# Attention opening: the keys' sine products are kept in the unused half of the rotated queries' buffer

## The chip, the cores and the metric

The kernel runs on one core of one Trainium2 chip. The metric is the device time of one execution in microseconds (us); lower is better.

## The reference

A network of two layers is computed for 256 tokens of width 1024, in fp32. The first layer mixes with a gated linear recurrence (HGRN2), the second with sparse attention (NSA); each is followed by a SwiGLU feed-forward stage, and every stage's input is modulated by the condition vector `c`. What matters here is the opening of the attention: shared keys and values are projected from one modulated input, queries from another; the selected and the window keys and all queries are normalized per head and rotated by position.

```python
def apply_rope(x, cos, sin):
    x1, x2 = jnp.split(x, 2, axis=-1)
    return jnp.concatenate([x1 * cs - x2 * sn, x2 * cs + x1 * sn], axis=-1)
...
ks = apply_rope(rms_norm(k_sel, k_norm[1]), cos, sin)
kw = apply_rope(rms_norm(k_win, k_norm[2]), cos, sin)
q = rms_norm(proj[..., :NSA_Q_WIDTH].reshape(B, S, NSA_HEADS, NSA_HEAD_DIM), q_norm)
q_rope = apply_rope(q, cos, sin)
```

## The kernel before, in words

Activations lie with features on the 128 partitions and the 256 tokens along the free axis. All weights are streamed from HBM in pieces of 1 MB: SyncE issues a load into one of four `raw` buffers (`issue`, L308) whenever one comes free. Each piece is split into two fp32r parts in `process`: ScalarE (ACT) casts the high part `wh` (L337), VectorE (DVE) subtracts to get the low part `wl` (L341); TensorE (PE) multiplies both (`mm3`, L551 to L553; `tok_steps`, L993 to L995). Activations are split in the same way into `h` high (ACT, L546) and `h` low (DVE, L547).

A rotation (`rotate`, L1260) needs x1 and x2 swapped between partitions. DVE computes a sine product into a tile `us` (L1265) and a cosine product straight into the target (L1266); four DMAs issued by GpSimd (POOL, L1269) then move `us` by 32 partitions and add it into the target. The target is `KR` for the two keys (branches 0 and 1) and `QR` for the four pairs of query projections 0 to 3, each of which fills one quarter of QR (two of its eight columns of 256 tokens). The tag `us` has two buffers; in the order of the program the users are key 0, key 1, query 0, query 1, query 2, query 3. A buffer comes free when its four DMAs are done. The names in the profile are `usk` and `usq`.

The attention stage (`nsa`, L1325) first projects the keys and values that need no later input, then builds the query input `hq` (`full_pair`, L1370), rotates the keys (L1371), and goes through the steps of `ORDER["nsa"]`: `q0` to `q3` are query projections with their rotation (`query`, L1382), `K` builds the input of the remaining values (L1408, whose `h` the values' matmuls `v` need), `c0` and `c1` the compressed blocks, `G` the gates, `R` the multiplication of KR by the keys' norms (L1323), `s0` to `s7` the scores (`attend_scores`, PE at L1584 reads QR and KR), `v0` to `v7` the products with the values, `a` parts of the modulation (`ada`, a DVE sum over a weight piece at L406).

Order of the work: the program is traced in the order above, and a planner then lays out every engine's instructions by priority and by when it reckons buffers and inputs to be free; `AHEAD` and `PRI` move steps forward or back in priority (`rot` has -75, `q0` has 80). Each engine works its list in order, so an instruction that waits holds all that stands behind it on that engine. Waits and buffer releases follow from the tiles that the instructions read and write.

Of the kernel before, what the change touches and what calls it, by code (L numbers as in the profile page):

```python
# [11 lines left out]
F32 = mybir.dt.float32  # L12
# [9 lines left out]
P = 128  # L22
S = 256
# [166 lines left out]
def first(name):  # L190

    def wrap(f):
        def g(self, *a, **k):
            n = PRI.get(name, 0)
            if not n:
                return f(self, *a, **k)
            with self.tc.high_priority(offset=n):
                return f(self, *a, **k)
        return g
    return wrap  # L200


class K:
# [1053 lines left out]
        return u, sq  # L1257

    @first("rot")
    def rotate(self, u, gain, kr, name):  # L1260

        nc = self.nc
        cs, sn = (self.c(n)[:, None, :].to_broadcast([P, 2, S]) for n in ("cos", "sin"))
        us = self.s2.tile([P, 2, S], F32, tag="us", bufs=2, name=f"us{name}")
        nc.vector.scalar_tensor_tensor(us, u, gain, sn, op0=ALU.mult, op1=ALU.mult)  # L1265
        nc.vector.scalar_tensor_tensor(kr, u, gain, cs, op0=ALU.mult, op1=ALU.mult)  # L1266
        for b in range(4):
            d, e = 32 * b, 32 * (b ^ 1)
            nc.gpsimd.dma_start(kr[d:d + 32], us[e:e + 32], accum_op=ALU.add)  # L1269
# [55 lines left out]
    def nsa(self):  # L1325
        nc = self.nc
        with self.tc.tile_pool(name="ns", bufs=1) as sp, self.tc.tile_pool(name="ns2", bufs=2) as s2, \
                ExitStack() as self.late:
            self.sp, self.s2 = sp, s2
            self.PC, self.Pt, self.RQ, self.rq = {}, {}, {}, None  # L1330
            self.rsel = sp.tile([P, 4 * P], F32R, name="rsel")
            rsel = s2.tile([P, 2, S], F32, tag="hsq", bufs=2, name="rselr").rearrange("p a b -> p (a b)")
            nc.sync.dma_start(rsel, self.a["rsel"])
            nc.scalar.copy(self.rsel, rsel)
            self.w2 = sp.tile([P, 2, 2, 64], F32, name="w2")
            nc.sync.dma_start(self.w2, self.a["w2"])

            def proj(name, i, h):
                ws = self.fetch(name, i, ahead=0)
                ps = self.acc_tile(f"{name}{i}")  # L1340
                for m in range(2):
                    self.gemm(ps[:, m], self.tiles(ws[m]), h[0], h[1])
                return ps

            KR = sp.tile([P, 2, 2, S], F32, name="KR")
            V = sp.tile([P, 2, 2, 256], F32, name="V")
            self.KR, self.V = KR, V
            Dt = [sp.tile([P, 2, 512], F32, tag=f"D{i}", name=f"D{i}") for i in range(2)]
            with ExitStack() as early:
                sk = early.enter_context(self.tc.tile_pool(name="nsk", bufs=1))  # L1350
                dk = []
                for kind in range(2):
                    dk.append(self.gemm_deferred(self.fetch("kv", kind), self.h, sk, f"kv{kind}", 3))
                kk = []
                for br in range(2):
                    sw, u = self.gemm_deferred(self.fetch("kv", 2 + 2 * br), self.h, sk, f"k{br}", 3)
                    sq = s2.tile([P, 2, S], F32, tag="hsq", bufs=2, name=f"hsqk{br}")
                    hu = s2.tile([P, 2, S], F32, tag="hu", bufs=2, name=f"huk{br}")
                    for m in range(2):
                        nc.scalar.activation(sq[:, m], u[:, m], AF.Square, bias=sw[:, m:m + 1])  # L1360
                        nc.scalar.activation(hu[:, m], u[:, m], AF.Identity, bias=sw[:, m:m + 1])
                    kk.append((hu, sq))
                self.load_late()
                while self.n_proc <= SCHED.index(("lin", "nq", 0)):
                    self.process()
                xr = sk.tile([P, KD, S], F32, name="xr")
                for m in range(0, KD, 2):
                    nc.vector.tensor_tensor(xr[:, m:m + 2], self.x[:, m:m + 2],
                                            self.rstd[:, None, :].to_broadcast([P, 2, S]), op=ALU.mult)
                hq = self.full_pair(1, 2, xr, s2, QACT)  # L1370
                for br in range(2):  # L1371
                    self.rotate(kk[br][0], self.col("k_norm", 1 + br), KR[:, :, br], f"k{br}")
                ks = [KR[:, :, br] for br in range(2)]
                rs = self.head_norm(kk)
                for kind in range(2):
                    self.cmp_blocks(*dk[kind], kind, Dt[kind], sk)
                self.QR = sp.tile([P, 8, S], F32, name="QR")

                self.QN, self.O, hk = {}, None, []
                qq, qd = {}, []  # L1380

                def query(i):  # L1382
                    if i == 2:
                        qd.append(sp.tile([P, 2, 2, S], F32, tag="D0", name="qd"))
                    qq[i] = self.raw_heads(proj("nq", i, hq), f"q{i}", qd[0][:, i % 2] if i > 1 else None)
                    self.rotate(qq[i][0], self.col("q_norm"), self.QR[:, 2 * i:2 * i + 2], f"q{i}")

                def query_norm(g):
                    pairs = [qq.pop(2 * g), qq.pop(2 * g + 1)]
                    self.QN[g] = [u for u, _ in pairs]  # L1390
                    self.row_norm(pairs, g)

                def values(br):
                    ps = self.acc_tile(f"v{br}")
                    self.gemm_tok(ps, hk[0], self.fetch("kv", 3 + 2 * br, ahead=0))
                    nc.scalar.copy(V[:, :, br], ps)

                comp = self.compress(Dt)
                for t in ORDER["nsa"]:
                    n = int(t[1:] or 0)  # L1400
                    ahead = AHEAD.get(t, 0)
                    with self.tc.high_priority(offset=ahead) if ahead else ExitStack():
                        if t[0] == "q":
                            query(n)
                        elif t[0] == "R":
                            self.head_mul(*rs, kk, ks)
                        elif t[0] == "K":
                            hk.append(self.full_pair(0, "kv", xr, s2, KACT))  # L1408
                            early.close()
                            self.s3 = self.late.enter_context(self.tc.tile_pool(name="nsp", bufs=PTS))  # L1410
                        elif t[0] == "G":
                            self.gates(hq)
                        elif t[0] == "c":
                            next(comp)
                        elif t[0] == "n":
                            query_norm(n)
                        elif t[0] == "w":
                            values(n)
                        elif t[0] == "x":
                            self.cmp_softmax(n)  # L1420
                        elif t[0] == "s":
                            self.attend_scores(n)
                        elif t[0] == "v":
                            if self.O is None:
                                self.O = self.h_tiles(0)
                            self.attend_values(n)
                        else:
                            self.adas(1)
            gate = self.need(("gate", 2))
            nxt = self.next_h(1, 3)  # L1430
            for i in range(4):
                ws = self.fetch("nsa_out", i)
                for m in range(2):
                    ps = self.acc_tile(f"nso{i}_{m}")
                    self.gemm_wide(ps, self.tiles(ws[m]), lambda k: self.h0[:, k, :, :S])
                    self.residual(ps[:, 0], 2 * i + m, gate, nxt, ps[:, 1])
            self.end_residual(nxt)
            self.h = nxt
# [331 lines left out]
```

## Time and profile before

| | us |
|---|---|
| median of 3 runs (lowest to highest) | 716.28 (715.77 to 716.33) |
| the profiled execution | 716.71 |
| its span | 714.9 |
| PE busy in the span | 696.8 |
| DVE busy in the span | 585.5 |
| ACT busy in the span | 429.6 |
| POOL busy in the span | 20.0 |

The span is the time from the first to the last recorded instruction of the profiled execution; 1.8 us of its time lie outside. PE stands for TensorE's matmuls, PEld for its weight loads, DVE for VectorE, ACT for ScalarE, POOL for GpSimd, SP for SyncE. A line is written L1265. Tiles carry the names of the program; `us` of the keys is `usk`, of the queries `usq`. The granted clock (PEclk) is the share of full speed that TensorE was given. The attention stage lies between about 357 and 500 us of the span.

### The profile page before, as it was taken

Reading aid. Unit: us, or ns where it says so; the run is one execution under the profiler, and the core shown is the slowest. Engines: PE = TensorE matmul, PEld = TensorE weight load, DVE = VectorE, ACT = ScalarE, POOL = GpSimd, SP = SyncE. Lnnn points to the kernel's source line nnn. Section 1 sums busy time; section 2 is a strip of 40 time slices with the busy share of each in tenths; the row PEclk is TensorE's granted clock in tenths of the full one; section 3 lists DMA queues with packets and bytes.
Section 4 is the critical chain, followed back from the end, with each engine's and each line's share of the span. In section 5 each row is a group of like instructions: output and inputs, shape, how many; then the busy total and the mean of one; then the engine's idle time right before and its main releaser. Section 6 shows DMA issues by size and latency. Waiting matters only on the chain.

```text
span 714.9 us, 13853 instructions
## 1 busy us (share of the span) xinstructions
PE 696.8 (97%) x5429; PEld 608.1 (85%) x5429; DVE 585.5 (82%) x1216; ACT 429.6 (60%) x855; POOL 20.0 (3%) x29
## 2 busy tenths in 40 slices
PE   7999999999999999999998599999999999999998
PEld 4998987999998888888897598555899888888887
DVE  6996986799999999999696589875899887686651
ACT  4669977667564665634375366779757665654330
POOL 0000000000000000000003130100000000000000
PEclk9999999999999999999999799999999999999999
DMA  8997768635499888997639463765455766564530
GB/s 354 425 423 296 256 273 301 250 119 196 171 354 363 327 309 311 354 347 278 248 108 315 124 204 122 251 235 178 177 184 182 276 242 215 202 254 161 200 125 23
DMA packets 28707, 174.00 MB, mean 243 GB/s; under 512 B 3297, under 2 KB 5217, under 8 KB 8930
## 3 DMA queue, kind: packets, MB, share of 16 engines
q1 hardware_dynamic: 26800, 170.80, 64.3%
q0 software_dynamic: 1408, 1.57, 1.8%
q8 instruction: 43, 0.70, 0.4%
q10 hardware_dynamic: 434, 0.74, 0.3%
q14 instruction: 22, 0.18, 0.1%
HBM read 170.48 MB, written 1.05 MB: 240 GB/s over the span
## 4 chain that ended last, share of the span: by engine, by line
PE 93%; DVE 3%; DMA 2%; ACT 1%; issue 0%; POOL 0%; DVEq 0%; POOLq 0%
PE ffo L563 11%; PE ff L563 9%; PE ffo L564 5%; PE ff L564 5%; PE po L1644 3%; PE ff L551 2%; PE ff L552 2%; PE ff L553 2%; PE s L1584 2%; PE adapsss L445 2%; PE nso L563 2%; PE ptt L1626 2%; DMA KR<-usk 2%; PE hg_g L551 1%; PE hg_i L993 1%; PE hgo L551 1%
## 5 line engine op out<-in xcount | busy, mean ns | idle before, releaser
L341 DVE TENSOR_TENSOR wl<-raw,wh 128x1024 fp32r<-128x1024 f32 x193 | 233.8, 1219 | 52.5 <-ACT wh L337 51.7
L337 ACT CAST wh<-raw 128x1024 fp32r<-128x1024 f32 x193 | 199.9, 1049 | 122.0 <-PE ffo L563 37.4
L563 PE MATMUL ffo<-g,wh 128*128 128x512 f32 x330 | 116.0, 394 | 0.0
L563 PE MATMUL ff<-h,wh 128*128 128x512 f32 x280 | 99.9, 395 | 0.0
L564 PE MATMUL ffo<-g,wl 128*128 128x256 f32 x330 | 93.0, 282 | 0.0
L406 DVE CUSTOM_DVE_ANT_0 junk<-raw,crep 128x1024 f32<-128x1024 f32 x68 | 82.7, 1216 | 0.1
L564 PE MATMUL ff<-h,wl 128*128 128x256 f32 x280 | 78.5, 280 | 0.0
L563 PEld LDWEIGHTS ffo<-g,wh 128*128 128x128 f32 x330 | 62.0, 188 | 14.5
L563 PEld LDWEIGHTS ff<-h,wh 128*128 128x128 f32 x280 | 52.8, 189 | 12.1 <-DVE h L740 0.2
L564 PEld LDWEIGHTS ffo<-g,wl 128*128 128x128 f32 x330 | 62.0, 188 | 0.0
L564 PEld LDWEIGHTS ff<-h,wl 128*128 128x128 f32 x280 | 52.8, 189 | 0.2
L551 PE MATMUL ff<-h,wh 128*128 128x258 f32 (+1 forms) x144 | 40.6, 286 | 0.0
L552 PE MATMUL ff<-h,wh 128*128 128x258 f32 (+1 forms) x144 | 40.4, 283 | 0.0
L553 PE MATMUL ff<-h,wl 128*128 128x258 f32 (+1 forms) x144 | 40.3, 283 | 0.0
L485 ACT ACTIVATE Pt<-Pt,nm,rq 128x128 f32<-128x128 f32 x64 | 34.2, 540 | 2.8 <-DVE nm L1594 2.8
L802 DVE SCALAR_TENSOR_TENSOR x<-ffo,mod,x 128x256 f32<-128x256 f32 x31 | 14.9, 481 | 16.6 <-PE ffo L564 11.5
L551 PEld LDWEIGHTS ff<-h,wh 128*128 128x128 f32 x144 | 27.0, 189 | 0.3
L552 PEld LDWEIGHTS ff<-h,wh 128*128 128x128 f32 x144 | 27.2, 189 | 0.0
L553 PEld LDWEIGHTS ff<-h,wl 128*128 128x128 f32 x144 | 27.1, 190 | 0.0
L563 PE MATMUL nso<-h,wh 128*128 128x512 f32 x64 | 22.4, 395 | 0.0
L1589 DVE CUSTOM_DVE_ANT_0 Pt<-s,cst 128x128 f32<-128x128 f32 (+1 forms) x64 | 19.5, 353 | 2.6 <-PE s L1584 2.4
L546 ACT CAST g<-fg 128x256 fp32r<-128x256 f32 x44 | 17.8, 404 | 6.1 <-DVE fg L1209 5.0
(496 smaller groups left out, 1800.2 us busy)
## 6 DMA issues: line engine op xcount, KB each, us to landing
raw<-in_w SPq DMA_DIRECT2D x147, 1024.0 KB, 5.0
raw<-in_w SPq DMA_DIRECT2D x11, 512.0 KB, 6.8
rawq<-in_w SPq DMA_DIRECT2D x3, 1024.0 KB, 9.4
rawv<-in_w SPq DMA_DIRECT2D x2, 1024.0 KB, 11.5
w1late<-in_w SPq DMA_DIRECT2D x2, 1024.0 KB, 5.9
x<-in_x SPq DMA_DIRECT2D x2, 512.0 KB, 4.9
rawv<-in_w SPq DMA_DIRECT2D x2, 512.0 KB, 8.4
QR<-usq POOLq DMA_DIRECT2D x16, 64.0 KB, 3.2
```

Of the source, the lines that this page charges most:

```text
L337: r = nc.scalar.copy(wh, u)
L341: r = nc.vector.tensor_tensor(wl, u, wh.bitcast(F32), op=ALU.subtract)
L406: r = nc.vector.tensor_tensor_reduce(out=junk, in0=t[:, h * D:(h + 1) * D], in1=self.crep, scale=1.0, scalar=0.0, op0=ALU.mult, op1=ALU.ad ...
L485: r = nc.scalar.activation(out, in_, func, **kw)
L546: self.nc.scalar.copy(hi, v)
L551: mm(ps, lhsT=wh, rhs=hh, start=first, stop=False)
L552: mm(ps, lhsT=wh, rhs=hl, start=False, stop=False)
L553: return mm(ps, lhsT=wl, rhs=hh, start=False, stop=last)
L563: mm(ps, lhsT=w[k][0], rhs=b, start=k == 0, stop=False)
L564: mm(ps[:, 0], lhsT=w[k][1], rhs=b[:, 0], start=False, stop=k == n - 1)
L1589: nc.vector.tensor_tensor_reduce(out=Pt[half][:, br, o:o + n], in0=ps[half][:, br], in1=cs[:, S - n:], scale=1.0, scalar=-3e38, op0=ALU.ad ...
L1644: done[half].append(nc.tensor.matmul(po[64 * half:64 * half + 64, t], lhsT=w[:, half], rhs=rhs, start=n == 0, stop=n == len(steps) - 1, ti ...
```

## The change

`rotate` takes an optional tile for the sine product. For the two keys it is given quarters 2 and 3 of QR (columns 4 to 5 for branch 0, 6 to 7 for branch 1), which are written for queries 2 and 3 only later; QR is therefore made ahead of the keys' rotation. The queries go on using the tag `us`.

```diff
     @first("rot")
-    def rotate(self, u, gain, kr, name):
+    def rotate(self, u, gain, kr, name, us=None):
...
-        us = self.s2.tile([P, 2, S], F32, tag="us", bufs=2, name=f"us{name}")
+        if us is None:
+            us = self.s2.tile([P, 2, S], F32, tag="us", bufs=2, name=f"us{name}")
         nc.vector.scalar_tensor_tensor(us, u, gain, sn, op0=ALU.mult, op1=ALU.mult)
         nc.vector.scalar_tensor_tensor(kr, u, gain, cs, op0=ALU.mult, op1=ALU.mult)
...
                 hq = self.full_pair(1, 2, xr, s2, QACT)
+                self.QR = sp.tile([P, 8, S], F32, name="QR")
                 for br in range(2):
-                    self.rotate(kk[br][0], self.col("k_norm", 1 + br), KR[:, :, br], f"k{br}")
+                    self.rotate(kk[br][0], self.col("k_norm", 1 + br), KR[:, :, br], f"k{br}",
+                                self.QR[:, 4 + 2 * br:6 + 2 * br])
...
-                self.QR = sp.tile([P, 8, S], F32, name="QR")
```

## Rows read from the trace of the kernel before

**Rows 1.** The page, busy time of each engine and its share of the span.
```profile
PE 696.8 (97%) x5429; PEld 608.1 (85%) x5429; DVE 585.5 (82%) x1216; ACT 429.6 (60%) x855; POOL 20.0 (3%) x29
```

**Rows 2.** Waits, 372 to 432 us: who waited for whom, total us, times, longest.
```profile
DVE usq L1265 <- DMA KR<-usk: 9.9, 1, 9.9
...
PE v L995 <- DVE h L547: 8.6, 1, 8.6
```

**Rows 3.** Table by stretches of 2 us: busy times, then PEclk, DMA share, GB/s.
```profile
396.00:398.00 2.00, 0.00 (x0) 0.00 (x0) 0.00 (x0) 0.00 (x0) 0.00 (x0) 0.58 1.03 366
...
402.00:404.00 2.00, 2.00 (x12) 2.00 (x11) 1.50 (x6) 2.00 (x7) 0.31 (x1) 0.50 0.66 66
...
406.00:408.00 2.00, 2.00 (x17) 2.00 (x16) 0.66 (x3) 0.18 (x1) 0.00 (x0) 0.86 0.00 0
...
412.00:414.00 2.00, 2.00 (x19) 2.00 (x18) 1.65 (x4) 1.64 (x3) 0.00 (x0) 1.00 1.02 410
```

**Rows 4.** Tile `usk`, 386 to 387 us: durations min/median/max in ns, starts, landings.
```profile
L1269 POOL DMA_DIRECT2D KR<-usk x4: 2159/2649/3144, 384.5 to 386.1; - x4
...
DMA to landing us min/median/max: 9.9/11.9/13.6
```

**Rows 5.** Timeline of DVE: start, us, instruction, idle time before it and its releaser.
```profile
385.86 0.74 DVE L1266 SCALAR_TENSOR_TENSOR QR<-huq,cols,cst 128x512 f32<-128x512 f32 x1
...
398.10 0.75 DVE L1265 SCALAR_TENSOR_TENSOR usq<-huq,cols,cst 128x512 f32<-128x512 f32 x1 [9.89 <-DMA KR<-usk]
398.77 1.22 DVE L341 TENSOR_TENSOR wl<-raw,wh 128x1024 fp32r<-128x1024 f32 x1
399.90 0.76 DVE L547 TENSOR_TENSOR h<-t,h 128x256 fp32r<-128x256 f32 x2
...
405.97 0.69 DVE L547 TENSOR_TENSOR h<-t,h 128x256 fp32r<-128x256 f32 x2
408.90 1.23 DVE L341 TENSOR_TENSOR wl<-raw,wh 128x1024 fp32r<-128x1024 f32 x1 [2.24 <-ACT wh L337]
...
415.82 1.22 DVE L406 CUSTOM_DVE_ANT_0 junk<-raw,crep 128x1024 f32<-128x1024 f32 x1
```

**Rows 6.** Timeline of ACT.
```profile
389.03 1.05 ACT L337 CAST wh<-raw 128x1024 fp32r<-128x1024 f32 x1 [1.28 <-DMA raw<-in_w]
390.61 0.71 ACT L546 CAST h<-t 128x256 fp32r<-128x256 f32 x2 [0.53 <-PE cmp L1477]
```

**Rows 7.** Timeline of PE.
```profile
391.54 0.28 PE L552 MATMUL nq<-h,wh 128*128 128x256 f32 x1
400.38 0.58 PE L995 MATMUL v<-wh,h 128*128 128x256 f32 x1 [8.56 <-DVE h L547]
...
406.66 0.28 PE L993 MATMUL v<-wh,h 128*128 128x256 f32 x1
406.78 0.28 PE L994 MATMUL v<-wl,h 128*128 128x256 f32 x1
```

**Rows 8.** Loads into `raw` issued at 387.5 and at 410.2 us, each with its landing.
```profile
L308 SPq DMA_DIRECT2D raw<-in_w x1: 548/548/548, 387.5 to 387.5; - x1
...
DMA to landing us min/median/max: 12.4/12.4/12.4
...
L308 SPq DMA_DIRECT2D raw<-in_w x1: 328/328/328, 410.2 to 410.2; - x1
...
DMA to landing us min/median/max: 4.9/4.9/4.9
```

**Rows 9.** Waits, 432 to 715 us: the largest in total.
```profile
DVE wl L341 <- ACT wh L337: 37.8, 41, 1.6
```

**Rows 10.** Chain that ended last at 428 us; tile `usq`, 428 to 428.8 us.
```profile
428.42 2.78 PE s L1584 x11
...
L1269 POOL DMA_DIRECT2D QR<-usq x3: 1057/1350/1690, 427.2 to 428.2; - x3
...
DMA to landing us min/median/max: 5.0/5.2/5.4
```

## The prediction

> **What bounds the kernel now.** First the page: TensorE (PE) is busy 97% of the span [rows 1], so a gain must come either from PE's few idle stretches or from stretches in which its clock is low. Then the list of waits of the attention's opening, 372 to 432 us: VectorE (DVE) stood 9.9 us in one single wait, ahead of the query's sine product (`usq`, L1265), released by a DMA that adds a key's sine product into KR; PE's largest wait there, 8.6 us, is for DVE's `h` at L547 [rows 2]. The table by stages shows the same hole from PE's side: the granted clock falls to 0.58 in 396 to 398 us, is 0.50 of full speed (1.2 of 2.4 GHz) while PE works at 402 to 404, and is back only in 406 to 408 (0.86, a mixed slice) [rows 3]. So one wait costs twice: the hole, and the slow matmuls behind it.
>
> Why the DMA is late: of the eight KR DMAs, the last four are issued at 384.5 to 386.1 us and land 9.9 to 13.6 us after [rows 4], beside the weight loads. The two `us` buffers hold the two keys' sine products until these DMAs have read them; the first query is the third user and must wait. Behind `usq` on DVE stand, in this order, the `wl` subtraction (L341) and the two `h` subtractions (L547) that PE needs [rows 5].
>
> **The change, part by part.**
> Removed: the two keys' claims on the `us` buffers. Their products go into quarters 2 and 3 of QR, which belong to queries 2 and 3; queries 0 and 1 then find both `us` buffers unused. Instructions, DMAs and their sizes stay as many as before. The `us` products keep their 128x512 shape, so 0.75 us each [rows 5].
>
> Step 1, the stall. DVE is free at 398.10 - 9.89 = 388.21 us [rows 5]. `usq` then ends at 388.96. The next one, `wl`, needs ScalarE's cast that runs 389.03 to 390.08 and itself waited for a weight load [rows 6], so 1.1 us of the 9.89 stays. `wl` starts at about 390.10 instead of 398.77: DVE gains 8.67 us. The `h` behind it needs the casts that start at 390.61 and take 0.71 for the pair [rows 6]; the first is done at about 391.0, `wl` at 391.3, so they add nothing. PE's L995 moves from 400.38 to 391.71; its matmul before it started at 391.54 and these start 0.12 apart [rows 7], so PE no longer stops at all.
>
> Step 2, the clock. From 400.38 to 406.66 PE starts 29 matmuls in 6.28 us (the second and third of [rows 7]); at the spacing right after, 0.12, they take 3.48. That gives 2.80 more, if nothing else holds PE. Their inputs come from the chain of `h` subtractions on DVE, 399.90 to 406.66 [rows 5], which moves by 8.67 and so ends at 398.0. Laying PE's 0.12 grid against it, each `h` chunk arrives within about 0.1 us of its turn: chunk 2 is due at 393.4 and ready at 393.35, chunk 7 due at 398.1 and ready at 398.0. I take the full 2.80; the other bound is 0 (PE paced by that chain).
>
> Behind that, DVE waits 2.24 us for a cast at 408.90 [rows 5], which PE's progress releases; that idle time takes up nearly all of the 2.80 by which PE gets ahead of DVE.
>
> Step 3, the moved DMAs. The query's four accumulating DMAs are issued behind the eighth KR DMA, which leaves GpSimd at 386.1 + 3.1 = 389.2 us [rows 4], rather than from 399; in the trace their transfers fill about 0.66 of the DMA engines for 4 us, from 400 to 404 (one of the two slices of 2 us stands in [rows 3]), about 2.6 us of all engines. They now share the engines with weight loads. The load issued at 387.5 landed after 12.4 us, at 399.9 [rows 8]; it may come 2.6 later, 402.5. The next load, issued at 410.2 when a buffer came free, took 4.9 us alone [rows 8]; DVE uses it in the L406 sum at 415.82 [rows 5]. All that moves 11.47 earlier: issue 398.7, use 404.35. The load lands between 403.6 (alone) and 407.4 (4.9 after 402.5), so DVE would wait 0 to 3.0 us there. At the 410 GB/s of a slice with such a load [rows 3], 1.05 MB behind 402.5 end at 405.05, 0.7 late; I take 0.4, since the 2.6 is a worst case.
>
> Queues passed: GpSimd has only these DMAs in the stretch; SyncE's loads keep their order. New waits: query 2's cosine product must wait until the keys' DMAs have read quarter 2; those landed by 399.7, and it stands two projections later, shortly before the first scores. The KR DMAs themselves are as late as before; what reads KR next is the product at L1323 and then the scores at 428.42 [rows 10], 417 after the shift, so some 17 us cover them and I take 0; without that cover the cost would be the 13.6 us of the landing at most.
>
> Nothing later gives it back to the weight stream: from 432 us to the end the waits are among engines (largest in [rows 9]), none for a DMA.
>
> Sum: 8.67 + 2.80 - 0.4 = 11.07 us against the profiled execution's 716.71, of which 1.8 us lie outside its span; the median of the runs is 0.43 lower, so 716.28 - 11.1 = **705.2 us**.
>
> **Rule against row.** The eight KR DMAs are 64 KB each (32 partitions x 512 x 4 bytes); the last landed 13.6 us after its issue, at 399.7 [rows 4]. The Trainium skill, page "DMA: Bandwidth & Descriptors", section on the anatomy of one DMA on the SWDGE path, puts such a DMA at about 2.0 us plus its bytes at 436 GB/s, an estimate of 2.15 us here. By that the last would land at 388.3, the stall would be 0.1 us and the change worth nothing. The trace disagrees, and the wait that I remove is the measured one.
>
> **The rivals.**
> (a) The clock's share is given back: PE is paced by the `h` chain, or by the L406 load of step 3, so that only DVE's 8.67 counts: **707.6 us**. For it: chunks arrive within 0.1 us of their turn. Against: DVE's 2.24 us of idle time behind them.
> (b) The order changes. Each engine's order is laid out by a planner that knows which buffers are free; with the first query's wait gone it may set `usq` earlier and others later. If two pairs of cast and `wl` (1.05 and 1.22 us, [rows 5, 6]) come that much later in front of PE: 2 x 2.27 = 4.5 us less gain, **709.8 us**. Against: the number of instructions is the same and only one starts freely.
> (c) There is nothing to remove: DVE meets the same DMAs at another instruction, or they land as the rule says and the stall was of one execution: **716.3 us**. Against: the wait is 9.9 us long, and its cause, the third use of two buffers, is in the code.
> (d) Slower, by one mechanism: accesses to QR are ordered over the whole buffer and not by region. Then the first query's cosine product, at 385.86 us [rows 5], must wait until the last KR DMA has read its quarter, 386.1 + 13.6 = 399.7 [rows 4]. The 2.35 us between 385.86 and 388.21 and `usq` then follow (0.67 from start to start): `wl` at 402.7 rather than 398.77, 3.95 more: **720.2 us**. It decides at the moment DVE reaches that product. Against: at 428.42 PE reads quarter 0 of QR for scores, while DMAs issued at 427.2 to 428.2 are adding into another quarter and land 5.0 to 5.4 us after [rows 10]; PE did not wait for them, so regions are told apart.
>
> **How the numbers follow.** Forecast 0.56, (a) 0.22, (b) 0.10, (c) 0.05, (d) 0.07. About 0.2% (1.4 us) can be told from no change here. Faster is forecast + (a) + (b) = 0.88, same 0.05, slower 0.07. The range reaches up to (b), 710, and down to 703: the forecast without the 0.4, less some 2 us, about one cast and `wl` pair of (b) set the other way. Outside it lie (c), (d) and the worse half of (b), some 0.17, and a little below.
>
> **What would show it.** Right: no wait of DVE over 2 us at `usq`; PE without a hole over 1 us between 388 and 400 us; granted clock 1.00 throughout there; `wl` about 390; first scores at about 417 instead of 428.4. Step 2 wrong: PE idle in many pieces of 0.1 to 0.5 us at v L995. Step 3 wrong: a wait of DVE L406 for `raw` over 1 us. Wrong altogether: DVE waiting on KR's DMAs at QR L1266, or a hole of several us elsewhere between 390 and 500 us.

## The result, and the profile after

The changed kernel takes **705.67 us** (median of 4 runs, 705.45 to 706.42) against 716.31 us for the kernel before (4 runs, 715.77 to 718.04): a ratio of 0.9849, 95% interval 0.9831 to 0.9868, so 10.6 us less. Forecast were 705.2 us and 11.1 us less. The profiled execution took 706.42 us with a span of 704.6 us; before it was 716.71 and 714.9, so that pair differs by 10.3.

Lines of `rotate` and of what stands below it have moved by one or two: the sine product is L1266, the cosine product L1267, the accumulating DMAs L1270, the scores L1586.

First the page, the row that answers to [rows 1]:

```profile
PE 694.4 (99%) x5429; PEld 605.6 (86%) x5429; DVE 585.1 (83%) x1216; ACT 429.9 (61%) x855; POOL 20.0 (3%) x29
```

Every engine has the same number of instructions and within 2.5 us the same work. What has gone is mostly idle time: before, PE was idle for 18.1 us of the span (714.9 - 696.8), now for 10.2.

Where it went is seen best by one stretch. The table by stretches for 386 to 412 us has, after the stretch, the sum and the busy time of PE, PEld, DVE, ACT and POOL (with the number of instructions that started), the granted clock, the DMA share and GB/s. The kernel before:

```profile
386.00:412.00 26.00, 17.44 (x127) 16.65 (x124) 11.36 (x22) 8.72 (x19) 6.43 (x8) 0.80 0.64 184
```

The changed kernel, the same stretch and two of the slices that answer to [rows 3]:

```profile
386.00:412.00 26.00, 26.00 (x220) 25.07 (x217) 21.00 (x45) 14.81 (x29) 7.84 (x12) 1.00 0.80 266
...
396.00:398.00 2.00, 2.00 (x17) 1.89 (x16) 1.99 (x5) 1.44 (x2) 0.00 (x0) 1.00 1.05 369
...
402.00:404.00 2.00, 2.00 (x19) 2.00 (x19) 1.01 (x1) 1.60 (x3) 0.00 (x0) 1.00 0.58 234
```

PE starts 220 matmuls where it started 127, is never idle, and keeps the full clock; at 396 it stood still at 0.58, at 402 it started 12 matmuls at 0.50, and now 19 at 1.00.

The cause is on DVE. Its timeline (start, us, instruction, idle time before it and its releaser), to hold against [rows 5]:

```profile
386.43 0.74 DVE L1266 SCALAR_TENSOR_TENSOR usq<-huq,cols,cst 128x512 f32<-128x512 f32 x1
...
387.29 0.74 DVE L1267 SCALAR_TENSOR_TENSOR QR<-huq,cols,cst 128x512 f32<-128x512 f32 x1
...
390.55 1.23 DVE L341 TENSOR_TENSOR wl<-raw,wh 128x1024 fp32r<-128x1024 f32 x1 [1.22 <-ACT wh L337]
391.69 0.42 DVE L537 TENSOR_SCALAR sg<-cmp 128x256 f32<-128x256 f32 x1
392.02 0.75 DVE L547 TENSOR_TENSOR h<-t,h 128x256 fp32r<-128x256 f32 x2
...
397.65 1.23 DVE L341 TENSOR_TENSOR wl<-raw,wh 128x1024 fp32r<-128x1024 f32 x1
...
399.12 0.75 DVE L547 TENSOR_TENSOR h<-t,h 128x256 fp32r<-128x256 f32 x2
...
402.99 1.23 DVE L341 TENSOR_TENSOR wl<-raw,wh 128x1024 fp32r<-128x1024 f32 x1 [1.72 <-ACT wh L337]
404.46 1.23 DVE L406 CUSTOM_DVE_ANT_0 junk<-raw,crep 128x1024 f32<-128x1024 f32 x1 [0.25 <-DMA raw<-in_w]
```

The query's sine product no longer waits for anything, and the `wl` behind it waits 1.22 us for the cast. Three things in the order of this stretch are new: the sine product has moved ahead of the cosine product (it was 12.24 us behind it), a step of the compressed blocks (`sg`, L537) stands ahead of the `h` subtractions, and the next `wl` (397.65) stands ahead of the last two of them (before, it came behind them, at 408.90 [rows 5]).

PE's timeline, for [rows 7]:

```profile
391.99 0.28 PE L551 MATMUL nq<-h,wh 128*128 128x256 f32 x1
...
392.34 0.28 PE L551 MATMUL nq<-h,wh 128*128 128x256 f32 x1
392.49 0.39 PE L995 MATMUL v<-wh,h 128*128 128x256 f32 x1
```

No bracket of idle time stands behind any of them. GpSimd's timeline shows the moved DMAs, and the tile QR how long they took to land (all twenty DMAs that read or write QR from 380 to 430 us: min, median and max):

```profile
382.43 7.04 POOL L1270 DMA_DIRECT2D KR<-QR  x8 [30.77 <-DVE KR L1267]
388.60 2.48 POOL L1270 DMA_DIRECT2D QR<-usq  x2
391.68 0.77 POOL L1270 DMA_DIRECT2D QR<-usq  x1 [0.60 <-DMA KR<-QR]
392.73 0.77 POOL L1270 DMA_DIRECT2D QR<-usq  x1 [0.29 <-DMA KR<-QR]
```

```profile
L1586 PE MATMUL s<-KR,QR x16: 375/534/694, 418.0 to 422.1; 64*128 64x256 f32 x8, 64*128 64x512 f32 x8
...
DMA to landing us min/median/max: 2.4/7.3/13.4
```

The keys' DMAs, the slowest of these, are as late as they were (13.4 us at most, 13.6 before [rows 4]). Only now nobody on DVE stands behind them; GpSimd itself waits for two of them, 0.60 and 0.29 us.

Three points on the way to the end, before and after: first scores 428.35 and 418.01 us (-10.3; the chain in [rows 10] takes them up at 428.42), first matmul of the attention's output projection 502.3 and 492.0 (-10.3), last output DMA 712.1 and 701.8 (-10.3). The attention of this execution of the changed kernel began 0.56 us later (its first `rb` matmul, L730, at 358.08, 357.52 before), an offset that is there in the first layer already, far ahead of the change (the program's first `rb` matmul at 173.1, 172.5 before). Without it the shifts are 10.9, 10.8 and 10.9. So the whole gain is made ahead of the scores, and nothing is given back behind them.

### The profile page after: what moved, and what is told of

It reads as the page before. It is cut to its first block, busy times and chain, and to the rows that moved or that the text cites. A ratio compares the mean times of both kernels' runs of the same rounds, so it can differ in the third digit from the quotient of the medians.

```text
span 704.6 us, 13851 instructions
## 1 busy us (share of the span) xinstructions
PE 694.4 (99%) x5429; PEld 605.6 (86%) x5429; DVE 585.1 (83%) x1216; ACT 429.9 (61%) x855; POOL 20.0 (3%) x29
## 4 chain that ended last, share of the span: by engine, by line
PE 96%; DVE 2%; ACT 1%; issue 0%; DMA 0%; DVEq 0%
PE ffo L563 11%; PE ff L563 9%; PE ffo L564 6%; PE ff L564 5%; PE po L1646 3%; PE ff L551 2%; PE ff L552 2%; PE ff L553 2%; PE s L1586 2%; PE adapsss L445 2%; PE nso L563 2%; PE ptt L1628 2%; PE hg_g L551 1%; PE hg_i L993 1%; PE hgo L551 1%; PE hg_i L995 1%
## 5 line engine op out<-in xcount | busy, mean ns | idle before, releaser
L406 DVE CUSTOM_DVE_ANT_0 junk<-raw,crep 128x1024 f32<-128x1024 f32 x68 | 82.7, 1216 | 0.4 <-DMA raw<-in_w 0.2
L551 PE MATMUL ff<-h,wh 128*128 128x258 f32 (+1 forms) x144 | 40.7, 286 | 0.0
L551 PEld LDWEIGHTS ff<-h,wh 128*128 128x128 f32 x144 | 27.1, 189 | 0.3
```

What stands on the lines that cost most here:

```text
L406: r = nc.vector.tensor_tensor_reduce(out=junk, in0=t[:, h * D:(h + 1) * D], in1=self.crep, scale=1.0, scalar=0.0, op0=ALU.mult, op1=ALU.ad ...
L551: mm(ps, lhsT=wh, rhs=hh, start=first, stop=False)
```

## The experiments

**One key in a tile of its own.** The changed kernel, but key 0's product gets its own tile, and key 1's goes back to the tag `us`. QR's unused half is not used at all.

```diff
-                                self.QR[:, 4 + 2 * br:6 + 2 * br])
+                                sk.tile([P, 2, S], F32, name="usk0") if br == 0 else None)
```

> The changed kernel, but only key 0's sine product leaves the tag us, and it goes into a tile of its own instead of QR; key 1 keeps a us buffer. Theory (the first query waited only because it was the third user of two buffers): one buffer free at that moment is enough and its place does not matter, so 705.7 us within 1.0, no wait of DVE over 1 us at the first query's sine product, no hole of PE over 1 us there. Rival (the gain needs both products out of us, or needs QR as their place): about half the gain, 711 us, with a wait of some 4 to 10 us moved to the second query's sine product.

Measured: 707.13 us against 716.79, ratio 0.9865 (0.9851 to 0.9880); the median lies 0.4 us above the 705.7 within 1.0 that was expected. The first scores start at 417.7 us and no wait of DVE for the keys' DMAs is left. In the profiled execution (705.8 us span) the next stage starts about 1 us later than after the change (493.1 for 492.0), and three rows of the table by stretches say where:

```profile
425.00:450.00 25.00, 24.33 (x175) 17.71 (x176) 22.03 (x75) 15.29 (x52) 1.78 (x4) 0.95 0.58 211
...
424.00:426.00 2.00, 2.00 (x12) 2.00 (x12) 1.92 (x6) 2.00 (x9) 0.00 (x0) 0.56 0.00 0
426.00:428.00 2.00, 2.00 (x13) 2.00 (x12) 2.00 (x7) 2.00 (x9) 0.00 (x0) 0.59 0.34 41
```

The changed kernel has the same 24.33 us of PE in that stretch, with 186 matmuls at a clock of 1.00. In the two short slices it starts 19 matmuls each at 1.00, where 12 and 13 start here. So the granted clock fell for some 3 us although PE was busy all the time, as it was in the 6 us before, in both kernels; why it fell here is open. Of this kernel's four executions the two with a mean granted clock of 0.998, the profiled one among them, took 707.6 and 707.8 us, the other two 706.4 and 706.7. What follows: it is the third user of two buffers that had to wait; that a buffer was found in QR saves memory, and the gain does not need it.

**One key in QR.** Half of the change: key 0's product in quarter 2 of QR, key 1's in the tag `us`.

```diff
-                                self.QR[:, 4 + 2 * br:6 + 2 * br])
+                                self.QR[:, 4:6] if br == 0 else None)
```

> The changed kernel, but only key 0's sine product lies in QR; key 1's stays in the tag us. Theory (third user of two buffers): the first query finds one free buffer, the second comes 20 us later, when key 1's DMAs have landed; 705.7 us within 1.0. Rival (both products must leave): the second query's sine product waits, time between 707 and 716 us.

Measured: 706.73 us against 716.79, ratio 0.9861 (0.9847 to 0.9876), at the edge of what was expected, with an interval that overlaps the whole change's (0.9831 to 0.9868) in good part; scores at 417.7. So one buffer set free gives the whole gain, as far as these runs can tell. The first query takes it, and the second, which is then the one to wait, comes after the DMAs have landed.

**The wait put back.** The changed kernel, with both keys in QR, but the first query's sine product also goes to quarter 2, where key 0's still lies.

```diff
-                    self.rotate(qq[i][0], self.col("q_norm"), self.QR[:, 2 * i:2 * i + 2], f"q{i}")
+                    self.rotate(qq[i][0], self.col("q_norm"), self.QR[:, 2 * i:2 * i + 2], f"q{i}",
+                                self.QR[:, 4:6] if i == 0 else None)
```

> The changed kernel with both keys' products in QR, but the first query's sine product is written into the quarter that holds key 0's, so it must again wait until key 0's DMAs have read it; nothing else differs. Theory (the wait is the cost): DVE stands 9 to 10 us at that product, PE has a hole of 8 to 9 us and works at the lower clock for some 6 us after it; 716.3 us within 1.0. Rival (the gain comes from another layout or from the order that the planner wrote for the new layout): it stays within 2 us of 705.7.

Measured: 715.53 us (10 runs) against 716.79, ratio 0.9984 (0.9975 to 0.9994). The list of waits, who waited for whom, total, times and longest:

```profile
DVE QR L1266 <- DMA KR<-QR: 8.9, 1, 8.9
...
PE v L995 <- DVE h L547: 7.5, 1, 7.5
```

and two slices of the table by stretches:

```profile
396.00:398.00 2.00, 0.00 (x0) 0.00 (x0) 1.08 (x2) 0.00 (x0) 0.03 (x1) 0.50 0.86 333
...
400.00:402.00 2.00, 2.00 (x11) 2.00 (x11) 1.31 (x4) 2.00 (x8) 1.14 (x2) 0.50 0.83 83
```

The wait, PE's hole and the half clock are back, each under its old name, and PE, ACT and DVE work in exactly their order of before. All but 1.3 us of the gain is gone. In the profiled execution (712.5 us span, the fastest of the ten) the wait itself is 1.0 us shorter than in [rows 2], because the DMAs landed earlier (12.9 us after their issue at most, 13.6 before), and the clock is back sooner (0.83 in 402 to 404 us, 0.50 in [rows 3]). This run shows the cause: with that one wait the changed program is as slow as before, but for those 1.3 us.

**The order of before.** In the changed kernel the planner put `usq` and `sg` elsewhere. Here the changed kernel gets ordering edges that bring DVE's order of before back exactly; 20 of PE's matmuls stand elsewhere in its list, and ACT's list differs in 4 places.

```diff
-        nc.vector.tensor_scalar_min(t, v, 0.0)
+        r = nc.vector.tensor_scalar_min(t, v, 0.0)
+        if shape == [P, 256]:
+            self.after(r, self.hl1)
...
+        if name == "q0":
+            self.after(r, self.last_hr)
...
```

> The changed kernel with two ordering edges on DVE, which put the first query's sine product and one step of the compressed blocks where the kernel before had them; DVE then has the order of before, PE and ACT nearly so, but no wait for the keys' DMAs. Theory (the stall and the clock behind it are the whole gain, the new order is neutral): 705.7 us within 0.8, granted clock 1.00 all through 388 to 410 us. Rival (the planner's new order carries a part): 707.5 us or more.

Measured: 706.12 us against 716.79, ratio 0.9855 (0.9838 to 0.9871). So the order is worth nothing that these runs can tell. DVE's list is here the same as in the run with the wait put back: the two differ by the wait, and by 9.4 us. Two slices of this execution are of use:

```profile
390.00:392.00 2.00, 2.00 (x19) 1.56 (x15) 0.00 (x0) 0.64 (x1) 1.75 (x3) 1.00 1.06 379
392.00:394.00 2.00, 0.77 (x5) 0.41 (x3) 1.56 (x3) 1.02 (x3) 1.38 (x2) 1.00 1.07 374
```

PE stands still for 1.2 us of the second. The list of waits for 385 to 400 us has ScalarE's cast waiting 2.8 us for a weight load, DVE's `wl` behind it, and PE's two waits that follow:

```profile
ACT wh L337 <- DMA raw<-in_w: 2.8, 1, 2.8
DVE wl L341 <- ACT wh L337: 2.8, 1, 2.8
...
PE v L999 <- DVE h L549: 0.7, 1, 0.7
PE v L997 <- ACT h L548: 0.6, 1, 0.6
```

The clock stays at 1.00 in every slice of 2 us from 386 to 412, and the first scores come at 419.50, 1.2 us later than after the change when the openings (358.33 and 358.08) are taken off. So two short holes of 0.6 and 0.7 us cost their own length and no more here, where one of 8.6 us [rows 2] cost the clock too.

**Short loads.** The kernel before, with nothing changed in its buffers, but four weight pieces that are in flight around the keys' DMAs are loaded with 128 of their 2048 columns only, which the casts then repeat (so the values computed from those pieces are others).

```diff
+SHORT = (("lin", "nq", 1), ("lin", "nq", 2), ("lin", "kv", 5), ("lin", "nq", 3))
...
+            elif (kind, name, i) in SHORT:
+                self.nc.sync.dma_start(t[:, :P], self.a["w"][self.n_dma, :, :P])
...
+                if (kind, name, i) in SHORT:
+                    u = t[:, None, :P].to_broadcast([P, 8, P])
...
```

> The kernel before, but of the four weight pieces that are loaded beside the keys' DMAs (query projections 1, 2, 3 and the second values) only the first 128 of 2048 columns are loaded, and these are repeated in the casts; 3.9 of 4.2 MB of loading are left out there, so those four projections are not the reference's. The keys' DMAs and the two us buffers are untouched. Theory (the keys' DMAs are late because they share the engines with weight loads): they land within 5 us of their issue, the wait of DVE falls below 2 us and the time to 705 to 707.5 us. Rival (they are late by themselves, eight accumulating DMAs behind one another): landings of 9 us and more stay, the wait stays above 6 us, the time above 712 us.

Measured: 706.30 us against 716.15, ratio 0.9861 (0.9842 to 0.9881). The tile `usk` and DVE's timeline:

```profile
L1279 POOL DMA_DIRECT2D KR<-usk x8: 995/2002/3149, 382.8 to 386.7; - x8
...
DMA to landing us min/median/max: 2.7/4.7/5.1
```

```profile
391.00 0.75 DVE L1275 SCALAR_TENSOR_TENSOR usq<-huq,cols,cst 128x512 f32<-128x512 f32 x1 [1.17 <-DMA KR<-usk]
```

With these loads cut the same eight DMAs land after 4.7 us in the median and 5.1 at most (9.4 and 13.6 in the kernel before), and the wait shrinks from 9.89 to 1.17 us. So it is the weight loads in flight beside them that make them late, and the wait, not the place of the products, is what costs. (The planner's order is another here too: a `wl` stands ahead of `usq`.) The Trainium skill, page "DMA: Bandwidth & Descriptors", section "Queues, rings and completion order", says that each DMA engine takes turns between the queues it has work for, packet by packet; landings that stretch beside other queues' loads agree with such a sharing, but no run shows the turns. The 2.15 us that the prediction worked out from the same page's fit are short even of these landings, 2.7 to 5.1 us.

**A filled hole, twice.** To price the clock by itself, PE got work for the hole: the kernel before, its wait kept, with matmuls of zeros ahead of the values' matmul that waits. First 64 of them:

```diff
...
+                if fill and tt == k == 0:
+                    z = self.pp.tile([P, 512], F32, tag="ada", bufs=1, name="fill")
+                    for _ in range(fill):
+                        with self.tc.high_priority(offset=2000):
+                            n = nc.tensor.matmul(z[:, :S], lhsT=self.zero, rhs=self.zero[:, :1].to_broadcast([P, S]), start=True, stop=True)
+                        self.after(n, r)
+                        r = n
...
```

> The kernel before, with 64 matmuls of zeros (128x256, into a spare PSUM bank) set in PE's order right before the values' matmul that waits for h, so that PE is busy in its hole; the wait of DVE stays as it is. The results are those of before. Theory (the stall costs twice, once as a hole and once through the clock behind it): the clock stays at 1.00 behind the hole and the 29 matmuls there start 0.12 us apart instead of 0.21; 713.5 us, between 712.9 and 714.5. Rival (the clock's share is hidden by the chain of h subtractions, which paces PE anyway): no change, 716.3 us within 0.6. If the fill takes longer than the hole, up to 0.5 us is lost.

Measured: 721.83 us against 716.15, ratio 1.0074 (1.0058 to 1.0091): slower, a miss. PE's timeline and two slices show why:

```profile
391.32 7.28 PE L1000 MATMUL fill<-zero 128*128 128x256 bf16 x64
```

```profile
400.00:402.00 2.00, 1.02 (x6) 0.82 (x6) 1.69 (x6) 1.23 (x4) 2.00 (x4) 1.00 0.65 66
...
404.00:406.00 2.00, 1.78 (x7) 1.28 (x6) 1.97 (x3) 1.54 (x4) 0.00 (x0) 0.50 0.00 0
```

The fill covers 391.3 to 398.6 us, but the planner had put the next query projection behind the values' matmuls (it starts at 410.98 us); in the kernel before, its matmuls stand among them. After the fill PE had only the values' matmuls, which wait for chunk after chunk of `h`, and the clock fell there instead. This run says nothing on the price asked for. So it was made again, with 72 matmuls and with edges that hold PE's list of before; ACT's is that of before too, and DVE's but for 3 places:

```diff
...
+    def fill_hole(self):
+        z = self.pp.tile([P, 512], F32, tag="ada", bufs=1, name="fill")
+        with self.tc.high_priority(offset=3000):
+            fill = [self.nc.tensor.matmul(z[:, :S], lhsT=self.zero, rhs=self.zero[:, :1].to_broadcast([P, S]), start=True, stop=True)
+                    for _ in range(FILL)]
+        seq, at = [], {c: iter(self.log[c]) for c in "gvqhkmc"}
+        for i, c in enumerate(MERGE):
+            if c == "v" and MERGE[:i].count("v") == 2:
+                seq += fill
+            seq.append(next(at[c]))
+        self.chain(*seq)
...
```

> The kernel before with 72 matmuls of zeros (128x256, bf16, into a spare PSUM bank) in PE's hole, and with ordering edges that keep PE's own matmuls there in the order of before; DVE and ACT have the order of before (one cast's partner moves by two places), the wait of DVE stays. The results are those of before. In the run with 64 of them and no edges the planner had moved the second query's projection behind the fill, so PE still starved and the clock fell later. Theory (the clock behind the hole costs 2.8 us): the clock stays at 1.00 from 390 to 410 us, the 29 matmuls behind the hole start about 0.12 us apart, 713.5 us, between 712.9 and 714.5. Rival (the chain of h subtractions paces PE there anyway, so the clock costs nothing by itself): 716.3 us within 0.6.

Measured: 715.14 us (11 runs) against 717.04, ratio 0.9973 (0.9964 to 0.9982), 1.9 us less (1.3 to 2.6): outside the 712.9 to 714.5 us that was expected, and clear of the rival's no change. Its waits, PE's timeline and two stretches:

```profile
DVE usq L1281 <- DMA KR<-usk: 9.5, 1, 9.5
```

```profile
391.93 8.17 PE L561 MATMUL fill<-zero 128*128 128x256 bf16 x72
400.27 0.39 PE L1010 MATMUL v<-wh,h 128*128 128x256 f32 x1 [0.17 <-DVE h L547]
```

```profile
402.00:404.00 2.00, 2.00 (x18) 2.00 (x18) 1.49 (x5) 2.00 (x7) 0.21 (x1) 1.00 0.67 74
...
450.00:475.00 25.00, 24.35 (x172) 13.51 (x171) 18.36 (x79) 17.96 (x61) 3.14 (x4) 1.00 0.65 210
```

The values' matmul comes as late as ever (400.27 for 400.38), DVE waits nearly as long as ever (9.5 for 9.9), and what differs is the clock: 18 matmuls in 402 to 404 us at 1.00 where there were 12 at 0.50 [rows 3]. The first scores start at 425.56 us, 2.8 earlier. From the values' matmul to the scores it is 25.3 us where it was 28.0, so the clock's term is 2.7 us there, nearly the 2.80 that was worked out. At the output projection 1.1 us are left (501.17 for 502.26). The 1.7 lost on that way are lost in one place, the modulation's matmuls at L445, whose weights this execution had to wait for (the kernel before had no such wait):

```profile
PEld adapsss L445 <- DMA raw<-in_w: 1.6, 1, 1.6
```

Ahead of that wait the same matmuls start 2.8 us earlier than in the kernel before (470.91 for 473.67), behind it 1.1 earlier (472.61 for 473.69), and so to the end. On PE 0.65 us of it shows as idle time, which is what the last row lacks to 25.

## Why the prediction was right

**Step 1, the stall (8.67 taken).** Right in kind and nearly in size. DVE's wait is gone, the cast takes 1.22 of it as forecast (1.1), `wl` starts at 390.55 (390.10 forecast, and 390.0 if the later opening of this execution, 0.56, is taken off). The values' matmul came 7.9 us earlier, 8.45 without the opening's 0.56; the planner now sets four query matmuls ahead of it where there were two (the first and the last of the four are the two at L551 above), which at 0.12 each is the missing 0.2.

**Step 2, the clock (2.80 taken).** Right in kind and nearly in size. The step was a difference of spacings (29 matmuls in 6.28 us, against 0.12 each); the second filled hole measured it with the wait in place: 2.7 us at the scores. The run with the old order measured it without the wait: from the values' matmul to the scores 25.4 us (394.06 to 419.50) where it was 28.0, so the chain of `h` subtractions does not pace PE in the old order either. Chunk 7's `h` is done at 399.87 (399.12 and 0.75), 1.9 us later than forecast (1.3 with the opening taken off), because a `wl` of 1.23 us now stands ahead of it; yet PE has no idle time from 386 to 412: in its list the query's matmuls, which need none of these chunks, stand between those that do. PE was not paced by that chain in the order that the planner chose, though the chunks themselves were not where the forecast had laid them.

**Step 3, the moved DMAs (0.4 taken).** Right on DVE, and without effect on PE: the weight load that the L406 sum uses was issued at 398.9 us (398.7 forecast) and took 5.5; the sum started at 404.46 (404.35 forecast) and waited 0.25. The last load ahead of it, issued at 388.1, took 13.2 us where its counterpart took 12.4 [rows 8]. But PE is busy without a gap up to the scores, so the trace shows nothing of the 0.4 on its path.

**The sum.** 11.07 forecast, 10.6 measured by the medians (9.5 to 12.1 by the interval), 10.9 at the scores by the trace. The remainder lies within the uncertainty of the runs. The table by stretches gives PE's account up to the first scores, from 386 us in the kernel before and, 0.56 later, in the changed one:

```profile
386.00:428.35 42.35, 33.78 (x263) 31.89 (x260) 26.59 (x53) 18.23 (x35) 11.24 (x16) 0.88 0.64 190
...
386.56:418.01 31.45, 31.45 (x265) 29.58 (x261) 26.45 (x53) 18.71 (x36) 9.19 (x12) 1.00 0.82 257
```

The 10.9 us are 8.6 of idle time and 2.3 of busy time. So the 0.4 of step 3 was not paid here, and of the 2.80 of step 2 some 0.5 is missing, about half of it because the new order has two more matmuls ahead of the scores; the rest is open. That these two errors nearly cancel in the sum is luck.

**The rivals.** (a), the clock's share given back: the change gains 10.9 at the scores and keeps 10.9 at the last output. The filled hole shows that such a loss can happen (1.7 of 2.8, at a late weight load), but the change did not suffer it. (b), another order: the planner did reorder, first of all at `usq`, and at no cost that the run with the old order can tell. (c), nothing to remove: refuted by the run with the wait put back. (d), ordering over the whole buffer: the first query's cosine product wrote quarter 0 at 387.29 us, while DMAs out of quarters 2 and 3, issued up to 386.3, had yet to land, up to 13.4 us after their issue. Regions are told apart here, as the scores in [rows 10] had suggested. GpSimd's two short waits for these DMAs are no sign against it: the run with key 0 in a tile of its own, with no key's product in QR, has one of 1.6 us.

## What to carry to other kernels

When an engine waits for a DMA to free a buffer, look first at who else may lend a buffer for that time: one buffer more was the whole gain as far as the runs can tell, and the DMA could stay as late as it was. Price such a wait on PE twice, by the hole and by the slow matmuls behind it at the granted clock of the table by stretches, and follow both to the first common point (here the scores). An experiment that adds work must hold the order of the rest, or it measures the planner.

## What the runs showed of the hardware that was not expected

- Eight accumulating DMAs of 64 KB landed 9.4 us after their issue in the median and 13.6 at most beside weight loads, and 4.7 and 5.1 us when those loads were cut to a sixteenth.
- Two holes of PE of 0.6 and 0.7 us left the clock at 1.00, one of 8.6 us was followed by 0.50, and with 72 matmuls of zeros in that hole it stayed at 1.00 throughout.
- The clock fell to 0.56 and 0.59 in two slices of 2 us, 424 to 428 us, in one execution (key 0 in a tile of its own), with PE busy all the time there and in the 6 us before, as in the changed kernel's execution at 1.00. No row shows the cause.
